# State space branch of a hybrid trunk: y and z with features on partitions instead of tokens

## The chip, the cores and the metric

The kernel runs on one core of one Trainium2 chip. The metric is the device time of one execution in microseconds (us). Three runs of the kernel before the change gave 2074.76, 2075.20 and 2075.37 us, a median of 2075.2.

## The reference

Two layers, each a mixer and a gated feed-forward, over 512 tokens of width 1024 in float32. The mixer has three branches (differential attention, latent attention and a state space branch), which read one normalised input `h`. The change touches the state space branch alone:

```python
xbc = silu(causal_dwconv(xbc, ssm_conv_w, ssm_conv_b))        # xs 1024, bm 4*128, cm 4*128
dt  = softplus(dt_raw + dt_bias);  a = -exp(a_log)            # 16 heads of 64, 4 groups of 4 heads
# per chunk of 128 tokens, cs = cumsum(dt * a) in the chunk
y_diag = ((cm @ bm.T) * exp(cs_l - cs_s) for s <= l) @ (xs * dt)
prev   = state left by the chunks before, decayed
y_off  = (cm @ prev) * exp(cs_l)
ys = y_diag + y_off + ssm_d * xs
ys = rmsnorm_per_group(ys * silu(z)) * ssm_norm               # over the 256 features of a group
# later: merged += sigmoid(gate_c) * (ys @ w_branch_c)
```

## The kernel before, in words

Activations that feed products lie with features on partitions (`hh`, `hl`: 8 tiles of 128 features x 512 tokens). Every float32 product is three products of a high and a low part (`mm3`, L145 to L147). Weights come in blocks of 1024 columns by one load on SP's queue (`wr`), ACT writes the high part (`wh`, L140) and DVE the low part (`wl`, L141); three of each are in turn. `lin_feat` gives a result with features on partitions: 48 wide products of 512 columns for 256 features. `lin_tok` gives it with tokens on partitions: 96 products of 256 columns (L224 to L226).

The branch loops over the 4 groups of heads (`for g in range(SSM_G)`). A group computes, in the order of the text: the x product and its convolution (L877 to L884, three DVE products for a tile, result `cv[0]`, `cv[1]`), the tail of the group before, the product for bm and cm with the same convolution (`cv[2]`, `cv[3]`), the z product, and then:

- `xdt`: x turned to tokens on partitions (L914) times dt; `y` starts as x times ssm_d (L920); bm turned (L926), `cb` = bm times cm (L931, L933), `xte` (L938) and the running states `prev` (L944 to L951)
- for each of 4 heads: the row of cs spread over partitions (L957), `dec` = min, exp (four ACT instructions) and times `cb`, then four y products (L965), one for each chunk of 128 tokens: stationary `dec` of 128 columns, moving `xdt` of 64
- the y products are added to `y`, three off products (L971, 256 columns) are scaled by exp(cs) and added, and `y` is multiplied by the gate of z (L977)
- the squares of `y` are summed along the free axis on ACT (L981), and `rstd_of` (L108 on DVE, L110 a power on POOL) gives one factor per token, that is per partition

The tail (`def tail`) scales `y` by that factor (L986, four instructions), turns `y` with eight transposes on PE (L990) and writes the parts `yh`, `yl` (L993, L994) from PSUM. The tail of group g is called between the x product and the bm and cm product of group g+1, the last one behind the first gate product of the merge.

In this branch a scheduler orders the instructions of each engine by costs of its own. Each engine then takes its queue strictly in that order. Wide products of the next group are put on PE between the small products of this one. Four PSUM banks serve the wide products and four the small ones (`mbank`, `abank`). Behind the branch follows the second attention, whose order on PE is written by hand: query and key products (L1082, L1104), wide products of the merge, and the transposes of queries and keys (L1123), which need DVE's and POOL's normalisation first.

Of the kernel before, what the change touches and what calls it, by code (L numbers as in the profile page):

```python
# [9 lines left out]
F32 = mybir.dt.float32  # L10
# [3 lines left out]
ALU = mybir.AluOpType  # L14
# [51 lines left out]
def trunk_kernel(ctx: ExitStack, tc: tile.TileContext, a: dict, out: bass.AP):  # L66
# [679 lines left out]
    def mix(l, x, hh, hl, ckr, cq, latp, scope):  # L746
# [51 lines left out]
        lss = small([P, T, 2], "lss", 1)  # L798
# [27 lines left out]
        scratch = ssd.tile([P, 256], F32, name="yo", bufs=2).rearrange("p (i t h) -> p i t h", i=4, t=T)  # L826
# [15 lines left out]
        nc.vector.tensor_tensor(out=da, in0=dt, in1=rv["a"].unsqueeze(1).broadcast_to([P, T, SSM_H]), op=ALU.mult)  # L842
        zeros = ssd.tile([P, S], F32, name="cb")
# [3 lines left out]
        cs, ncs, tot, ecs, te = (ssd.tile([P, T, SSM_H], F32, name=nm) for nm in ("cs", "ncs", "tot", "ecs", "te"))  # L847

        def decays():
# [13 lines left out]
            nc.scalar.activation(ecs.rearrange(flat), cp[:, 0:n16], AF.Exp)  # L863
# [6 lines left out]
        with ssd_scope:  # L870
            tails = []
            for g in range(SSM_G):
# [80 lines left out]
                yps = [abank().rearrange("p (c d) -> p c d", c=2) for _ in range(2)]  # L953
                for r in range(4):
                    h = 4 * g + r
                    lp_ = abank()
                    nc.tensor.matmul(lp_, sel[:, h:h + 1].broadcast_to([P, P]), cs_r, start=True, stop=True)  # L957
                    dec = sp.tile([P, T, P], F32, name="dec", bufs=3)
                    nc.vector.tensor_tensor(out=dec, in0=lp_.rearrange("p (c l) -> p c l", c=T),
                                            in1=cs[:, :, h:h + 1].broadcast_to([P, T, P]), op=ALU.min)  # L960
                    for c in range(T):
                        nc.scalar.activation(dec[:, c], dec[:, c], AF.Exp, bias=ncs[:, c, h:h + 1])
                    nc.vector.tensor_tensor(out=dec, in0=dec, in1=cb.rearrange("p (c d) -> p c d", c=T), op=ALU.mult)
                    for c in range(T):
# [623 lines left out]
```

## Time and profile before

| | us |
|---|---|
| median of three runs | 2075.2 |
| the profiled execution | 2072.72 |
| its span | 2071.0 |
| PE busy | 2043.1 |
| DVE busy | 1418.6 |
| ACT busy | 913.8 |
| POOL busy | 137.1 |

A busy PE is not a PE at its peak: its instructions overlap, so that what one costs is read from the distance of starts. The granted clock of TensorE over the span was 0.996. The branch takes two stretches of the span, about 84 to 290 us and about 1100 to 1290 us.

### The profile page before, as it was taken

The numbers are of one execution on the slowest core, as the hardware profiler recorded it, in microseconds if no ns is written. First come the engines' busy times: TensorE is split into PE (matmuls) and PEld (weight loads), VectorE is DVE, ScalarE is ACT, GpSimd is POOL, SyncE is SP. The second block draws the span as 40 slices with busy tenths as digits, with TensorE's granted clock in tenths as the row PEclk, the third lists the DMA queues.
The fourth block names the chain that finished last, engine by engine and source line by source line (L and its number), as shares of the span: only waits on it lengthen the run. The fifth ranks groups of instructions, "written<-read, shape, count | busy, mean of one in ns | idle before, by whom it ended". The sixth has DMA issues, their size and how long they took to land.

```text
span 2071.0 us, 30143 instructions
## 1 busy us (share of the span) xinstructions
PE 2043.1 (99%) x11469; PEld 1769.7 (85%) x11469; DVE 1418.6 (68%) x2742; ACT 913.8 (44%) x1683; POOL 137.1 (7%) x162
## 2 busy tenths in 40 slices
PE   8999999999999999999999999999999999999999
PEld 7888987789888988888898888888998898888888
DVE  7788887756876678658757888775566566553553
ACT  6744445535533454224434544454444335432441
POOL 4200011002100000000000000110020000000000
PEclk8999999999999999999999999999999999999999
DMA  8523232233445255655443223212333243323222
GB/s 268 150 69 85 78 116 90 87 108 113 152 153 169 94 187 165 196 179 166 153 141 85 79 62 89 64 48 79 93 93 93 92 133 92 102 92 102 92 92 82
DMA packets 224542, 237.20 MB, mean 115 GB/s; under 512 B 16126, under 2 KB 195742, under 8 KB 224142
## 3 DMA queue, kind: packets, MB, share of 16 engines
q1 hardware_dynamic: 221646, 232.63, 36.3%
q0 software_dynamic: 2752, 2.65, 0.5%
q8 instruction: 90, 1.47, 0.3%
q14 instruction: 54, 0.44, 0.1%
HBM read 226.30 MB, written 8.91 MB: 114 GB/s over the span
## 4 chain that ended last, share of the span: by engine, by line
PE 87%; DVE 7%; DMA 2%; POOL 2%; issue 2%; ACT 1%; SPq 0%; POOLq 0%; DVEq 0%; ACTq 0%
PE mb L145 22%; PE mb L147 21%; PE mb L146 21%; PE mb L224 3%; PE mb L226 3%; PE mb L225 3%; PE ab L965 1%; DVE wl L141 1%; PE mb L666 1%; PE ab L1140 1%; PE ab L1177 1%; DVE macc L522 1%; PE ab L1326 1%; PE ab L1082 1%; POOL r_r L110 1%
## 5 line engine op out<-in xcount | busy, mean ns | idle before, releaser
L145 PE MATMUL mb<-hh,wh 128*128 128x512 f32 (+1 forms) x1376 | 538.2, 392 | 1.8 <-DVE g L778 0.9
L147 PE MATMUL mb<-hh,wl 128*128 128x512 f32 (+1 forms) x1376 | 532.4, 387 | 0.0
L146 PE MATMUL mb<-hl,wh 128*128 128x512 f32 (+1 forms) x1376 | 531.3, 386 | 0.0
L141 DVE TENSOR_TENSOR wl<-wr,wh 128x1024 fp32r<-128x1024 f32 (+2 forms) x312 | 374.9, 1203 | 193.8 <-ACT wh L140 192.5
L140 ACT ACTIVATE wh<-wr 128x1024 fp32r<-128x1024 f32 (+2 forms) x312 | 324.7, 1042 | 338.4 <-PE mb L146 260.5
L147 PEld LDWEIGHTS mb<-hh,wl 128*128 128x128 f32 x1376 | 258.4, 188 | 51.7
L145 PEld LDWEIGHTS mb<-hh,wh 128*128 128x128 f32 x1376 | 258.3, 188 | 51.8 <-DVE g L778 1.8
L146 PEld LDWEIGHTS mb<-hl,wh 128*128 128x128 f32 x1376 | 258.8, 188 | 49.1 <-DVE hl L702 1.2
L1423 DVE SCALAR_TENSOR_TENSOR fu<-mb,vec,fu 128x510 f32<-128x510 f32 (+1 forms) x176 | 129.8, 745 | 90.5 <-ACT fu L1421 88.9
L224 PE MATMUL mb<-wh,hh 128*128 128x256 f32 x640 | 180.1, 281 | 0.0
L226 PE MATMUL mb<-wh,hl 128*128 128x256 f32 x640 | 178.6, 279 | 0.0
L225 PE MATMUL mb<-wl,hh 128*128 128x256 f32 x640 | 178.5, 279 | 0.0
L145 PE MATMUL mb<-gh,wh 128*128 128x512 f32 (+1 forms) x432 | 151.2, 350 | 0.0
L147 PE MATMUL mb<-gh,wl 128*128 128x512 f32 (+1 forms) x432 | 150.6, 349 | 0.0
L146 PE MATMUL mb<-gl,wh 128*128 128x512 f32 (+1 forms) x432 | 150.5, 348 | 0.0
L1421 ACT ACTIVATE fu<-mb,vec 128x512 f32<-128x512 f32 x88 | 67.9, 774 | 149.7 <-PE mb L147 149.7
L224 PEld LDWEIGHTS mb<-wh,hh 128*128 128x128 f32 x640 | 120.0, 188 | 1.2 <-ACT wh L140 0.4
L225 PEld LDWEIGHTS mb<-wl,hh 128*128 128x128 f32 x640 | 120.1, 188 | 0.4
L226 PEld LDWEIGHTS mb<-wh,hl 128*128 128x128 f32 x640 | 120.2, 188 | 0.0
L522 DVE SCALAR_TENSOR_TENSOR macc<-wg,c_act,macc 128x512 f32<-128x512 f32 x140 | 104.6, 747 | 20.0 <-DMA wg<-in_ada_w_dram 19.2
L145 PE MATMUL mb<-yh,wh 128*128 128x512 f32 x256 | 104.5, 408 | 0.9 <-ACT g L769 0.9
L147 PE MATMUL mb<-yh,wl 128*128 128x512 f32 x256 | 100.3, 392 | 0.0
(333 smaller groups left out, 3373.9 us busy)
## 6 DMA issues: line engine op xcount, KB each, us to landing
wr<-in_w_in_dram SPq DMA_DIRECT2D x88, 512.0 KB
wr<-in_ffn_w_up_dram SPq DMA_DIRECT2D x88, 512.0 KB
wg<-in_ada_w_dram SPq DMA_DIRECT2D x160, 256.0 KB
wr<-in_ffn_w_down_dram SPq DMA_DIRECT2D x40, 512.0 KB
wr<-in_w_in_dram SPq DMA_DIRECT2D x64, 256.0 KB
wm<-in_ada_w_dram SPq DMA_DIRECT2D x16, 512.0 KB
wr<-in_w_branch_c_dram SPq DMA_DIRECT2D x16, 512.0 KB
wr<-in_w_out_dram SPq DMA_DIRECT2D x16, 512.0 KB
```

Source lines behind the costliest of these rows:

```text
L110: nc.gpsimd.tensor_tensor(out=r, in0=ms, in1=nhalf[:, 0:1].broadcast_to([P, n]), op=ALU.pow)
L140: nc.scalar.activation(hi, raw[:, 0:n], AF.Copy)
L141: nc.vector.tensor_tensor(out=lo, in0=raw[:, 0:n], in1=hi, op=ALU.subtract)
L145: nc.tensor.matmul(o, lh, rh, start=first, stop=False)
L146: nc.tensor.matmul(o, lh, rl, start=False, stop=False)
L147: nc.tensor.matmul(o, ll, rh, start=False, stop=last)
L224: nc.tensor.matmul(o, hh[:, kk, ts_], wh[:, sl], start=first and k == 0, stop=False)
L225: nc.tensor.matmul(o, hh[:, kk, ts_], wl[:, sl], start=False, stop=False)
L226: nc.tensor.matmul(o, hl[:, kk, ts_], wh[:, sl], start=False, stop=last and k == 3)
L522: ins = nc.vector.scalar_tensor_tensor(out=acc[0], in0=rk, scalar=c_act[:, kk:kk + 1], in1=acc[0], op0=ALU.mult, op1=ALU.add)
L1421: nc.scalar.activation(u, bank, AF.Identity, bias=v[:, V_FCB + ti:V_FCB + ti + 1], scale=tap(2))
L1423: nc.vector.scalar_tensor_tensor(out=u[:, s_:], in0=bank[:, 0:S - s_], scalar=tap(2 - s_), in1=u[:, s_:], op0=ALU.mult, op1=ALU.add)
```

## The change

- The z product goes through `lin_feat`; `sz` has features on partitions, in one buffer instead of two.
- `y` has features on partitions. It no longer starts from the turned x; ssm_d comes in as a scalar per partition (`dcol`).
- Heads are taken in pairs. Of a y product the stationary side is now `xdt` (64 columns), the moving side `dec` (128 columns); the two heads of a pair write partitions 0 to 63 and 64 to 127 of one bank. The off product has `prev` as its stationary side, six products of 128 columns for three of 256. exp(cs) is taken from the spread row (`grow`).
- The factor of the norm is per token, which is now the free axis. The squares are summed over partitions by four products with a column of ones; the factor, again one per token with tokens on partitions, is written to DRAM (`r_d`, 512 numbers of 4 bytes) and read back spread over all partitions (`rows_`, 256 KB), both by POOL's queue. The second load waits for the first.
- The tail multiplies `y` by `rows_` and the norm's weight and splits it. It has no transposes.
- A few small tiles are made larger, so that tiles behind them keep their places.

```diff
@@ -840,11 +840,16 @@
+        dcol = ssd.tile([P, 64], F32, name="dcol")[:, 0:SSM_H // 2]
+        for r in range(2):
+            own = slice(r * SSM_HD, (r + 1) * SSM_HD)
+            nc.vector.tensor_copy(out=dcol[own], in_=rv["dvec"][own].rearrange("p (j r) -> p j r", r=2)[:, :, r])
...
@@ -898,28 +902,24 @@
-                sz = sp.tile([P, T, 256], F32, name="sz", bufs=2)
-
-                def ev_z(tt, bank):
-                    o = sz[:, 2 * tt:2 * tt + 2]
+                sz = sp.tile([P, 2, S], F32, name="sz")
+
+                def ev_z(i, bank):
+                    o = sz[:, i]
                     nc.scalar.activation(o, bank, AF.Tanh, scale=0.5)
                     nc.vector.scalar_tensor_tensor(out=o, in0=o, scalar=1.0, in1=bank, op0=ALU.add, op1=ALU.mult)
-                lin_tok(w_in, [(C_Z + 256 * g, 256)], hh, hl, ev_z)
+                lin_feat(w_in, (C_Z + 256 * g, C_Z + 256 * g + P), KT, h_rhs, ev_z)
...
-                    nc.vector.tensor_tensor(out=y[:, :, sl].rearrange("p c (r d) -> p c r d", r=2), in0=tv,
-                                            in1=rv["dvec"][:, hs].unsqueeze(1).unsqueeze(3).broadcast_to([P, T, 2, SSM_HD]),
-                                            op=ALU.mult)
...
@@ -950,48 +950,58 @@
-                for r in range(4):
...
-                    for c in range(T):
-                        nc.tensor.matmul(yps[c // 2][:, c % 2, r * SSM_HD:(r + 1) * SSM_HD], dec[:, c],
-                                         xdt[:, c, r * SSM_HD:(r + 1) * SSM_HD], start=True, stop=True)
+                for i in range(2):
+
+                    dec = sp.tile([P, 2, S], F32, name="dec", bufs=2)
+                    grow = sp.tile([P, S], F32, name="yo", bufs=2)
+                    for r in range(2):
...
+                        nc.tensor.matmul(lp_, sel[:, h:h + 1].broadcast_to([P, P]), cs_r, start=True, stop=True)
...
+                        nc.scalar.activation(grow[own, P:S], lp_[own, P:S], AF.Exp)
...
+                    nc.vector.tensor_tensor(out=dec, in0=dec, in1=cb.unsqueeze(1).broadcast_to([P, 2, S]), op=ALU.mult)
+                    yp = abank()
                     for c in range(T):
...
+                        for r in range(2):
+                            own = slice(r * SSM_HD, (r + 1) * SSM_HD)
+                            nc.tensor.matmul(yp[own, cs_], xdt[:, c, i * P + r * SSM_HD:i * P + (r + 1) * SSM_HD], dec[:, r, cs_],
+                                             start=True, stop=True)
+                    op_ = abank()
+                    for c in range(1, T):
+                        cs_ = slice(c * P, (c + 1) * P)
+                        nc.tensor.matmul(op_[:, cs_], prev[:, c - 1, i * P:(i + 1) * P], cmT[:, cs_], start=True, stop=True)
+                    nc.vector.tensor_tensor(out=grow[:, P:S], in0=grow[:, P:S], in1=op_[:, P:S], op=ALU.mult)
+                    j = 2 * g + i
+                    nc.vector.scalar_tensor_tensor(out=y[:, i], in0=cv[i], scalar=dcol[:, j:j + 1], in1=yp, op0=ALU.mult, op1=ALU.add)
+                    nc.vector.tensor_tensor(out=y[:, i, P:S], in0=y[:, i, P:S], in1=grow[:, P:S], op=ALU.add)
+                nc.vector.scalar_tensor_tensor(out=y, in0=y, scalar=0.5, in1=sz, op0=ALU.mult, op1=ALU.mult)
+                sq = [sp.tile([P, S], F32, name="yo", bufs=2) for _ in range(2)]
                 for i in range(2):
...
+                    nc.scalar.activation(sq[i], y[:, i], AF.Square)
+                nc.vector.tensor_tensor(out=sq[0], in0=sq[0], in1=sq[1], op=ALU.add)
+                ssp = abank()
                 for c in range(T):
-                    jk = sp.tile([P, 256], F32, name="yo", bufs=2)
-                    nc.scalar.activation(jk, y[:, c], AF.Square, accum_out=ss[:, c:c + 1])
-                r_ = rstd_of(ss, T, 256.0, "yn")
+                    nc.tensor.matmul(ssp[:, c:c + 1], sq[0][:, c * P:(c + 1) * P], ones[:, 0:1], start=True, stop=True)
+                r_ = rstd_of(ssp[:, 0:T], T, 256.0, "yn")
+
+                r_d = dram.tile([1, S], F32, name=f"r_d{l}{g}")
+                nc.gpsimd.dma_start(out=r_d.rearrange("o (c p) -> p (o c)", p=P), in_=r_)
+                rows_ = sp.tile([P, S], F32, name="u", bufs=3)
+                nc.gpsimd.dma_start(out=rows_, in_=r_d.broadcast_to([P, S]))
+
+                def tail(g=g, y=y, rows_=rows_):
                     for i in range(2):
-                        tp = abank()
-                        for c in range(T):
-                            nc.tensor.transpose(out=tp[:, c * P:(c + 1) * P], in_=y[:, c, i * P:(i + 1) * P], identity=ident)
+                        cw = col(V_SN + 2 * g + i)
+                        nc.vector.scalar_tensor_tensor(out=y[:, i], in0=y[:, i], scalar=cw, in1=rows_, op0=ALU.mult, op1=ALU.mult)
                         yh, yl = y_tiles()
...
+                        nc.scalar.activation(yh, y[:, i], AF.Copy)
+                        nc.vector.tensor_tensor(out=yl, in0=y[:, i], in1=yh, op=ALU.subtract)
                         ys.append((yh, yl))
```

How the instructions stand, at three places. DVE, first layer, from the gating of `y` of the first group to its tail (`u`, `cv`: convolution of the next group; `yn_ms`: input of the power on POOL; `yl`: low part of the result). Before:

```order
L977 SCALAR_TENSOR_TENSOR y<-y,sz 128x1024 [waits DVE_49]
L879 SCALAR_TENSOR_TENSOR u<-mb,vec_89,u 128x511 [waits Activation_49] x2
L879 SCALAR_TENSOR_TENSOR u<-mb,vec_89,u 128x510 [waits DVE_49]
L108 TENSOR_SCALAR yn_ms<-yss 128x4 [waits Activation_49]
L879 SCALAR_TENSOR_TENSOR u<-mb,vec_89,u 128x510 [waits DVE_49]
L879 SCALAR_TENSOR_TENSOR u<-mb,vec_89,u 128x509 [waits DVE_49] x2
L986 TENSOR_SCALAR y<-y,yn_r 128x256 [waits Pool_49]
L884 SCALAR_TENSOR_TENSOR cv<-cv,u 128x512 [waits Activation_49]
L986 TENSOR_SCALAR y<-y,yn_r 128x256 x3
L884 SCALAR_TENSOR_TENSOR cv<-cv,u 128x512 [waits Activation_49]
L141 TENSOR_TENSOR wl<-wr,wh 128x1024 [waits DMAHW3_49,PE_49]
L994 SCALAR_TENSOR_TENSOR yl<-ab,vec_89,yh 128x512 [waits Activation_49] x2
```

And now, where L1001 is the product of the tail (its `u` is the buffer of `rows_`) and DMASW the queue of POOL's loads:

```order
L983 SCALAR_TENSOR_TENSOR y<-y,sz 128x1024 [waits DVE_49]
L987 TENSOR_TENSOR yo<-yo 128x512 [waits Activation_49]
L108 TENSOR_SCALAR yn_ms<-ab 128x4 [waits PE_49]
L141 TENSOR_TENSOR wl<-wr,wh 128x1024 [waits DMAHW5_49,Activation_49]
L883 SCALAR_TENSOR_TENSOR u<-mb,vec_89,u 128x511 [waits Activation_49] x2
L883 SCALAR_TENSOR_TENSOR u<-mb,vec_89,u 128x510 [waits DVE_49] x2
L883 SCALAR_TENSOR_TENSOR u<-mb,vec_89,u 128x509 [waits DVE_49] x2
L1001 SCALAR_TENSOR_TENSOR y<-y,vec_89,u 128x512 [waits DMASW1_49]
L888 SCALAR_TENSOR_TENSOR cv<-cv,u 128x512 [waits Activation_49] x2
L1004 TENSOR_TENSOR yl<-y,yh 128x512 [waits Activation_49]
L1001 SCALAR_TENSOR_TENSOR y<-y,vec_89,u 128x512
```

Six convolution products and one `wl` stand between the norm's input L108 and the first instruction that waits for the load; the convolutions' second halves and the parts `yl` stand behind it.

POOL's queue in the first layer, before:

```order
L110 TENSOR_TENSOR lat_r<-lat_ms,nhalf 128x8 [waits DVE_49]
L110 TENSOR_TENSOR yn_r<-yn_ms,nhalf 128x4 [waits DVE_49] x3
L110 TENSOR_TENSOR yn_r<-yn_ms,nhalf 128x4 [waits DVE_49,Pool_49]
L1134 AFFINE_SELECT cmask<-sb 128x512 [waits DMAHW1_49,DMAHW2_49,DVE_49,PE_49]
L110 TENSOR_TENSOR r_r<-r_ms,nhalf 128x4 [waits DVE_49] x3
```

Now:

```order
L110 TENSOR_TENSOR lat_r<-lat_ms,nhalf 128x8 [waits DVE_49]
L110 TENSOR_TENSOR yn_r<-yn_ms,nhalf 128x4 [waits DVE_49]
L994 DMA r_d_1698<-yn_r 128x4x1 [waits DMASW0_49,Pool_49]
L996 DMA u<-r_d_1698 128x512 [waits DMASW1_49,DMAHW6_49,DMASW0_49,Activation_49]
L110 TENSOR_TENSOR yn_r<-yn_ms,nhalf 128x4 [waits DVE_49]
```

Behind each power stand the write to DRAM and the load from it, and the load waits for the write.

DVE behind the last group of the first layer, where the second attention begins (`Cq`: a table of the rotation). Before:

```order
L108 TENSOR_SCALAR yn_ms<-yss 128x4 [waits Activation_49]
L986 TENSOR_SCALAR y<-y,yn_r 128x256 [waits Pool_49]
L986 TENSOR_SCALAR y<-y,yn_r 128x256 x3
L141 TENSOR_TENSOR wl<-wr,wh 128x1024 [waits DMAHW3_49,PE_49,Activation_49]
L994 SCALAR_TENSOR_TENSOR yl<-ab,vec_89,yh 128x512 [waits Activation_49] x2
L1043 TENSOR_TENSOR Cq<-cos,w32q 128x4x16
```

Now:

```order
L108 TENSOR_SCALAR yn_ms<-ab 128x4 [waits PE_49,Pool_49]
L522 SCALAR_TENSOR_TENSOR macc<-wg,c_act,macc 128x512 [waits DMAHW7_49,DVE_49]
L141 TENSOR_TENSOR wl<-wr,wh 128x1024 [waits DMAHW4_49,PE_49,Activation_49]
L522 SCALAR_TENSOR_TENSOR macc<-wg,c_act,macc 128x512 [waits DMAHW1_49,DVE_49]
L522 SCALAR_TENSOR_TENSOR macc<-wg,c_act,macc 128x512 [waits DMAHW2_49,DVE_49]
L1001 SCALAR_TENSOR_TENSOR y<-y,vec_89,u 128x512 [waits DMASW7_49]
L1001 SCALAR_TENSOR_TENSOR y<-y,vec_89,u 128x512
L1004 TENSOR_TENSOR yl<-y,yh 128x512 [waits Activation_49] x2
L1053 TENSOR_TENSOR Cq<-cos,w32q 128x4x16
```

The wait for POOL alone has become a wait for POOL's load, and the attention's work on DVE stands behind it.

## Rows read from the trace of the kernel before

**Rows 1.** The page, busy time of each engine, its share, instructions.

```profile
PE 2043.1 (99%) x11469; PEld 1769.7 (85%) x11469; DVE 1418.6 (68%) x2742; ACT 913.8 (44%) x1683; POOL 137.1 (7%) x162
```

**Rows 2.** Windows, one group: us, busy (instructions) of each engine, PEclk, DMA share, GB/s.

```profile
170.78:214.12 43.34, 43.34 (x269) 38.81 (x268) 36.63 (x60) 21.02 (x44) 1.38 (x1) 1.00 0.27 74
```

**Rows 3.** The chain in order of time (start us, us, what), first layer.

```profile
126.14 0.87 PE ab L914 x8
170.78 0.87 PE ab L914 x8
175.85 1.29 PE ab L944 x6
214.12 0.87 PE ab L914 x8
```

**Rows 4.** Timeline of PE (start us, us, line, out<-in, shapes), the same group.

```profile
180.42 1.00 PE L965 MATMUL ab<-xdt,dec 128*128 128x64 f32 x8
189.42 0.39 PE L145 MATMUL mb<-hh,wh 128*128 128x512 f32 x1
...
198.53 0.39 PE L146 MATMUL mb<-hl,wh 128*128 128x512 f32 x1
202.65 0.28 PE L224 MATMUL mb<-wh,hh 128*128 128x256 f32 x1
208.30 0.28 PE L224 MATMUL mb<-wh,hh 128*128 128x256 f32 x1
```

**Rows 5.** Timeline of PE, products on column halves in the second attention.

```profile
344.79 1.09 PE L1177 MATMUL ab<-pT,vv 128*64 128x128 f32 x16
345.81 1.13 PE L1104 MATMUL ab<-wm,lat 128*128 128x256 f32 x4
```

**Rows 6.** Timeline of PE, sums over partitions by products with ones.

```profile
696.20 0.28 PE L147 MATMUL mb<-mh,wl 128*128 128x256 f32 x1
696.68 0.36 PE L145 MATMUL mb<-mh,wh 128*128 128x256 f32 x1
```

**Rows 7.** Timeline of DVE in the same group.

```profile
175.85 1.22 DVE L141 TENSOR_TENSOR wl<-wr,wh 128x1024 fp32r<-128x1024 f32 x1
188.89 1.29 DVE L968 TENSOR_TENSOR y<-y,ab 128x512 f32<-128x512 f32 x2 [1.88 <-PE ab L965]
196.37 0.16 DVE L108 TENSOR_SCALAR yn_ms<-yss 128x4 f32<-128x4 f32 x1
198.03 0.35 DVE L986 TENSOR_SCALAR y<-y,yn_r 128x256 f32<-128x256 f32 x1 [0.24 <-POOL yn_r L110]
205.05 2.71 DVE L879 SCALAR_TENSOR_TENSOR u<-mb,vec,u 128x510 f32<-128x510 f32 x4
210.74 0.69 DVE L884 SCALAR_TENSOR_TENSOR cv<-cv,u 128x512 f32<-128x512 f32 x1
```

**Rows 8.** The instructions of two tiles: bias_d, then c.

```profile
L670 POOL DMA_DIRECT2D bias_d<-ob x16: 691/735/938, 18.6 to 71.5; - x16
DMA to landing us min/median/max: 4.2/5.8/14.7
...
L474 SPq DMA_DIRECT2D c<-in_c_dram x1: 406/406/406, 0.8 to 0.8; - x1
L476 PEld LDWEIGHTS ab<-ident,c x1: 178/178/178, 2.4 to 2.4; 8*128 8x128 f32 x1
```

**Rows 9.** Timeline of PE, then DVE, behind the last group, first layer.

```profile
275.79 0.48 PE L147 MATMUL mb<-hh,wl 128*128 128x512 f32 x1
303.18 0.42 PE L1123 MATMUL ab<-ident,kn 128*96 128x128 f32 x2 [0.63 <-DVE kn L1116]
...
287.69 0.21 DVE L1043 TENSOR_TENSOR Cq<-cos,w32q 128x64 f32<-128x64 f32 x1
289.93 1.75 DVE L522 SCALAR_TENSOR_TENSOR macc<-wg,c_act,macc 128x512 f32<-128x512 f32 x2
```

**Rows 10.** Windows, a stretch ahead of the branch.

```profile
40.00:48.00 8.00, 5.58 (x26) 4.82 (x25) 7.93 (x22) 6.01 (x15) 4.57 (x5) 0.80 0.66 180
```

More of the change, by code (lines that the diff above doesn't have):

```diff
@@ L795, in mix @@
         sp = ssd = ssd_scope.enter_context(tc.tile_pool(name=f"ssd{l}", bufs=1, reuse_waits="tile"))
-        lss = small([P, T, 2], "lss", 1)
+        lss = small([P, 8 * T], "lss", 1)[:, 0:2 * T].rearrange("p (t k) -> p t k", k=2)
         krss = small([P, T], "krss", 2)
@@ L825, in mix @@
         dt = ssd.tile([P, T, SSM_H], F32, name="dt")
-        scratch = ssd.tile([P, 256], F32, name="yo", bufs=2).rearrange("p (i t h) -> p i t h", i=4, t=T)
+        scratch = ssd.tile([P, S], F32, name="yo", bufs=2)[:, 0:256].rearrange("p (i t h) -> p i t h", i=4, t=T)
         e, z2, poly = scratch[:, 0], scratch[:, 1], scratch[:, 2]
@@ L846, in mix @@
         nc.vector.tensor_copy(out=cs_r, in_=zeros)
-        cs, ncs, tot, ecs, te = (ssd.tile([P, T, SSM_H], F32, name=nm) for nm in ("cs", "ncs", "tot", "ecs", "te"))
+        cs, ncs, tot, te = (ssd.tile([P, T, SSM_H], F32, name=nm) for nm in ("cs", "ncs", "tot", "te"))
         def decays():
@@ L914, in mix @@
                         nc.tensor.transpose(out=tp[:, c * P:(c + 1) * P], in_=cv[i][:, c * P:(c + 1) * P], identity=ident)
-                    tv = tp.rearrange("p (c r d) -> p c r d", c=T, r=2)
                     hs = slice(4 * g + 2 * i, 4 * g + 2 * i + 2)
-                    sl = slice(i * P, (i + 1) * P)
-                    nc.vector.tensor_tensor(out=xdt[:, :, sl].rearrange("p c (r d) -> p c r d", r=2), in0=tv,
+                    nc.vector.tensor_tensor(out=xdt[:, :, i * P:(i + 1) * P].rearrange("p c (r d) -> p c r d", r=2),
+                                            in0=tp.rearrange("p (c r d) -> p c r d", c=T, r=2),
                                             in1=dt[:, :, hs].unsqueeze(3).broadcast_to([P, T, 2, SSM_HD]), op=ALU.mult)
-                    nc.vector.tensor_tensor(out=y[:, :, sl].rearrange("p c (r d) -> p c r d", r=2), in0=tv,
-                                            in1=rv["dvec"][:, hs].unsqueeze(1).unsqueeze(3).broadcast_to([P, T, 2, SSM_HD]),
-                                            op=ALU.mult)
                 bmt = sp.tile([P, T - 1, P], F32, name="bmt")
@@ L967, in mix @@
-                for i in range(2):
-                    nc.vector.tensor_tensor(out=y[:, 2 * i:2 * i + 2], in0=y[:, 2 * i:2 * i + 2], in1=yps[i], op=ALU.add)
-                for c in range(1, T):
-                    op_ = abank()
-                    nc.tensor.matmul(op_[:, 0:256], cmT[:, c * P:(c + 1) * P], prev[:, c - 1], start=True, stop=True)
-                    yo = sp.tile([P, 256], F32, name="yo", bufs=2)
-                    nc.vector.tensor_tensor(out=yo.rearrange("p (r d) -> p r d", r=4),
-                                            in0=op_[:, 0:256].rearrange("p (r d) -> p r d", r=4),
-                                            in1=ecs[:, c, hd].unsqueeze(2).broadcast_to([P, 4, SSM_HD]), op=ALU.mult)
-                    nc.vector.tensor_tensor(out=y[:, c], in0=y[:, c], in1=yo, op=ALU.add)
```

28 lines of the change are left out of this document (9 added, 19 removed).

## The prediction

> **What bounds the kernel now.** I began with the busy times of the engines: the reader is to see that PE is busy 99% of the span and no other engine more than 68% [rows 1]. Then I cut out one group of heads of the first layer. In its 43.34 us PE is busy for 43.34, DVE for 36.63, ACT for 21.02 and POOL for 1.38, at a granted clock of 1.00 [rows 2]. The chain of waits confirms it: from one turn of x (L914) to the next, the chain consists of PE alone, and the distance is 44.64 us to the second group and 43.34 to the third [rows 3]. So each microsecond less on PE is a microsecond of time, as long as nothing else becomes late, and DVE, which works 85% of the group, is the first that could.
>
> **What the change saves on PE**, per group, in steps.
> - The turns of y: eight transposes. Eight of the same shape (L914) take 0.87 [rows 3]. Saved: 0.87.
> - The z product: 96 products of 256 columns become 48 of 512. Of the former, 48 lie between 202.65 and 208.30, 0.1177 each, so 11.30 in all. Of the latter, 40 lie between 189.42 and 198.53, 0.228 each, so 10.93 [rows 4]. Saved: 0.37.
> - The block of y products runs from 180.42 to 189.42 [rows 4] and holds 15 wide products and three spread rows of cs, which are as wide: 18 x 0.228 = 4.10. The remaining 4.90 are y and off products. In their place come two sets of eight products on the two column halves. The second attention has eight of this kind: 344.79 to 345.81, that is 1.02 [rows 5], so 2.04. Six off products of 128 columns stand for three of 256: I take the six of L944, 1.29 [rows 3]. With 0.4 for changes of form between them that is 3.73. Saved: 1.17.
> - The sums of squares: four products with ones. In the normalisation of the feed-forward such sums stand between products 0.48 apart (696.20 to 696.68) that take 0.12 without them, so 0.36 [rows 6]. I count it twice, for the return to wide products. Added: 0.72.
>
> That is 1.7 less for a group, about 41.65 instead of 43.34. With eight groups it would be −13.5, if nothing waited. DVE loses its two products with ssm_d and some small pieces (about 1.4 of 36.6 per group), and ACT gains about 0.8 by the exps of the spread row; it has half of the group free [rows 2], which hides that.
>
> **What the change adds: a way through DRAM.** Before, the factor is ready for its user on DVE 1.66 after the norm's input (L108 at 196.37, L986 at 198.03 [rows 7]). Now, behind the same power on POOL, come a write to DRAM, a load that waits until it has landed, and then L1001 on DVE. On DVE's queue L1001 stands ahead of the second halves of the convolutions of the next group's bm and cm, of both parts of y, of the z gate, of xdt and of xte. PE needs bm's convolution for L926 and xte for L944. So if the load comes late, DVE stands, and after it PE.
>
> How late is late? Let D be the two landings together, from the write's issue to the load's arrival, and let time zero be the end of the last y product.
> - Off products (0.64), twenty wide products (4.55) and a hop of 0.1 bring PE to the sums at 5.3. They end at 6.1, L108 starts at 6.25, the power is done at 7.9, and the rows are there at 7.9 + D.
> - DVE's six convolution products and a low part of weights behind L108 take 6 x 0.67 + 1.15 (four of L879 in 2.71, a last one being 0.7; wl 1.22 with its overlap [rows 7]), so DVE reaches L1001 at 11.4. It waits from D = 3.5 on.
> - From L1001 to the end of xte stand 13 products of 512 columns at 0.60 (two in 1.29, one alone 0.69 [rows 7]), six of the convolution, 4.0, one low part, 1.15, and three pieces of xte, 1.05 (a piece of 256 columns takes 0.35 [rows 7]): 14.0. So xte is ready at 21.9 + D, with a hop 22.0 + D.
> - Then PE has, up to the next time zero: L944 1.29, two spread rows and hop 0.55, 24 wide 5.47, the first y products 1.02, off products 0.64, spread rows 0.55, 24 wide 5.47, hop 0.1, y products 1.02: 16.1.
>
> The period is the longer of 41.65 and 38.1 + D. It costs nothing up to D = 3.5, and is worse than 43.34 from D = 5.2 on.
>
> **How large is D?** No transfer of before goes to DRAM and straight back. The nearest row is POOL's other write of small blocks, bias_d: sixteen of them land 4.2 us after issue at the least, 5.8 in the middle, 14.7 at most [rows 8], at the start of the kernel, where the DMA engines are 0.66 busy (180 GB/s [rows 10]). In a group they are 0.27 busy (74 GB/s [rows 2]). So I take the least twice: D = 8.4. From below, the nearest row is the first transfer of SP: c, issued at 0.8 and used at 2.4 [rows 8], at most 1.6, on idle engines, for a few rows; twice that is 3.2. From above, the median of bias_d twice is 11.6. Less than nothing it can't be, since the load waits for the write.
>
> The Trainium skill (DMA: Bandwidth & Descriptors, section "Anatomy of one DMA — SWDGE (gpsimd) path") gives a transfer issued by POOL a fixed part of about 2.0 us and the bytes at 436 GB/s on top; for 2 KB and 256 KB that is an estimate of 2.0 + 2.6 = 4.6, and the period would be 42.7, shorter than before, the time 2069. The landings of bias_d in this trace are at least twice its fixed part, so I hold to them; the other case is the first rival.
>
> **The sum.** With D = 8.4 the period is 46.5: +1.9 at the first boundary (44.64) and +3.2 at each of the other two, +8.3 for a layer. The first group gains its share before time zero, −1.6. Behind the last group it is the attention that waits: PE's L1123 needs the keys, and the whole chain on DVE that makes them, from the rotation's tables at 287.69 to 303.18 [rows 9], now stands behind L1001. Before, L1123 came 27.4 after the last y product (275.79). Now 29 wide products stand ahead of the sums, so L108 is at 8.3, the power at 9.95, the rows at 9.95 + D, the tail takes 2.7, and the chain 12.0 (15.5 less two `macc`, 1.75, and two low parts, 1.7, which have moved ahead or aside): 24.65 + D, +5.7 at D = 8.4. PE would reach L1123 at about 22 and wait some 11. Together +12.4 a layer, 4D − 21.3 in general, and even at D = 5.3. Two layers: +24.8.
>
> The profiled execution took 2072.72 (span 2071.0), 2.5 below the median of the three runs. 2072.72 + 24.8 = 2097.5, on the median 2100.
>
> Costed at nothing: POOL's queue stands while it waits between its two transfers, but POOL has 1.38 us of work in a group, the power itself; only the norms of the attention's queries and keys stand behind it, and these wait for DVE anyway. The issue on POOL (0.7 a transfer [rows 8]) lies inside the landing times. SP loads the same bytes of z's weights in the same number of loads.
>
> **Rivals.**
> - Quick landing, D under 4.8. For it: the loads in the group have nearly idle DMA engines. Against it: bias_d. At D = 3.2 the layer gives −1.66 for three periods, −1.6 for the first group and about +0.5 for the attention's chain: −6.1, in all −12, 2063. It decides below D = 5.3.
> - Even, D from 4.8 to 5.8: the gain on PE and the new wait cancel, within 4 us, 2075.
> - The clock falls in the new gaps. With D = 8.4 PE stands for some 3 us ahead of L926 and 1 ahead of L944 in each group. In an early stretch PE is busy 5.58 of 8 us and the granted clock is 0.80 [rows 10], 1.6 us lost. For it: gaps of about the size. Against: two gaps in 46 us are less than there. One such loss for each of the eight waits, 13 us more: 2113.
> - The column halves don't run beside each other here. Two sets of eight cost 1.02 more each, 16 us in all: 2116. The attention's eight [rows 5] speak against it.
>
> **How the numbers follow.** Forecast 0.45, quick landing 0.23, even 0.10, the clock 0.18, the halves 0.04. Within 0.2% (4 us, about what a measurement of this kernel can tell from no change) is the even case, 0.10; faster is the first rival, 0.23; the rest is slower, 0.67. The range goes from the low bound of D to the high one: 4 x 11.6 − 21.3 = +25.1 a layer, +50, 2125, a little more for the clock: 2064 to 2128. With the forecast alone (D from 6.5 to 11) it is 2085 to 2121.
>
> **What would show it.** The wait of DVE at L1001 for the load, D − 3.5 = 4.9 us in each of six groups, longer in the last ones; waits of PE at L926 for `cv` and at L944 for `xte`, together about 4.8; one of some 11 at L1123 for `kn` in each layer; the period of L914 at 46.5. On the side of the gain: eight y products in 1.02, wide z products 0.228 apart, the sums in 0.72. I am wrong if the write and the load land within 5 us together, or if L1001 waits and PE does not, because the scheduler's order gives it enough to do.

## The result and the profile after

| | us | ratio to before | 95% interval |
|---|---|---|---|
| before | 2074.98 | | |
| after | 2170.05 (2168.49 to 2171.58, four runs) | 1.0459 | 1.0441 to 1.0477 |

The change makes the kernel 95 us slower; 25 were forecast, and the range ended at 2128. The profiled execution took 2169.62, 96.9 more than that of before. The page of after begins with PE, as in [rows 1]:

```profile
PE 2056.7 (95%) x11133; PEld 1751.9 (81%) x11133; DVE 1412.1 (65%) x2690; ACT 922.1 (43%) x1665; POOL 150.8 (7%) x178
```

PE is busy 13.6 us longer than before and stands 83 us more: the loss is waiting. Where it waits is read by stretches of the first layer, from the end of the last y product of one group to that of the next, and from the last one to the first turn of the queries (window, length, busy time of PE, PEld, DVE, ACT, POOL, granted clock, DMA share, GB/s):

```profile
146.41:199.37 52.96, 45.76 (x240) 37.58 (x238) 35.90 (x53) 23.92 (x45) 3.35 (x3) 0.94 0.25 65
199.37:253.02 53.65, 44.83 (x226) 36.36 (x224) 35.73 (x53) 22.07 (x42) 2.40 (x3) 0.90 0.23 64
253.02:307.91 54.89, 45.73 (x228) 36.61 (x226) 35.18 (x53) 23.15 (x44) 3.35 (x3) 0.91 0.22 63
307.91:350.93 43.02, 24.89 (x111) 20.88 (x110) 20.90 (x54) 8.75 (x15) 7.48 (x8) 0.76 0.40 96
```

Three periods of 52.96, 53.65 and 54.89 stand where one took 43.34 (44.64 the first) [rows 2, 3], and the end takes 43.02 where it was 25.9 (275.8 to 301.7). PE is idle for 7 to 9 us of each period and for 18 of the end, and the granted clock is below 1.00 in every one.

At the boundaries between groups the mechanism is the one forecast. Timeline of DVE at the first boundary (start us, duration us, what; in brackets the idle time before and who ended it):

```profile
168.47 0.75 DVE L1001 SCALAR_TENSOR_TENSOR y<-y,vec,u 128x512 f32<-128x512 f32 x1 [8.20 <-DMA u<-r_d]
181.48 1.08 DVE L938 TENSOR_TENSOR xte<-xdt,te 128x256 f32<-128x256 f32 x3
```

L1001 waits 8.20 us for the load, and from its start to the end of `xte` (182.5) go 14.1 us; 14.0 were forecast from [rows 7]. PE behind it, at the turn of bm and at the running states:

```profile
178.12 0.88 PE L926 MATMUL ab<-ident,cv 128*128 128x128 f32 x3 [6.34 <-DVE cv L888]
182.96 1.46 PE L944 MATMUL ab<-xte,bmt 128*128 128x256 f32 x6
```

PE waits at L926 for the convolution, as foreseen, and not at L944: DVE's last piece of `xte` ends just ahead of it. The steps of the boundary are those forecast; what differs is D, the time from the write's issue to the rows' arrival. The new way on POOL:

```profile
155.43 0.83 POOL L994 DMA_DIRECT2D r_d<-yn_r  x1 [0.29 <-POOL yn_r L110]
164.19 0.59 POOL L996 DMA_DIRECT2D u<-r_d  x1 [7.92 <-DMA r_d<-yn_r]
```

The write is issued at 155.43, the load, when the write has landed, at 164.19, and L1001 starts at 168.47: D is 13.0. Over all eight groups, instructions and landing times of the write (L994) and the load (L996):

```profile
L994 POOL DMA_DIRECT2D r_d<-yn_r x8: 801/806/833, 155.4 to 1372.7; - x8
DMA to landing us min/median/max: 8.2/9.0/10.6
...
L996 POOL DMA_DIRECT2D u<-r_d x8: 556/558/586, 164.2 to 1383.8; - x8
DMA to landing us min/median/max: 3.9/4.3/7.3
```

The load lands in 4.3, near the 4.2 that I took from bias_d [rows 8]. The write, of 2 KB, needs 9.0. In the six boundaries D is 13.0 to 14.0 (8.4 forecast, 11.6 the upper bound). For most of the write's time the trace records no packet, of it or of anything else: the last one ends at 157.63, and the write lands at 163.6. The packets from 157.7 to 164:

```profile
DMA packets 0, 0.00 MB, mean 0 GB/s; under 512 B 0, under 2 KB 0, under 8 KB 0
```

What passes in those 6 us no run shows. The trace may not record every piece on POOL's way, since e2_16byte, with a quarter of the pieces, has as many packets; e3_sp, on SP's, shows the pieces themselves.

The end of the branch, first layer. POOL's timeline:

```profile
318.62 0.81 POOL L994 DMA_DIRECT2D r_d<-yn_r  x1 [0.29 <-POOL yn_r L110]
329.71 0.56 POOL L996 DMA_DIRECT2D u<-r_d  x1 [10.28 <-issue]
```

SP's queue, from a pair of loads `wg` to the first of `wm`:

```profile
321.94 4.76 SPq L512 DMA_DIRECT2D wg<-in_ada_w_dram  x2
326.75 3.42 SPq L1078 DMA_DIRECT2D wm<-in_mla_w_uq_dram  x1
```

DVE, at the tail of the last group:

```profile
337.04 1.41 DVE L1001 SCALAR_TENSOR_TENSOR y<-y,vec,u 128x512 f32<-128x512 f32 x2 [14.34 <-DMA u<-r_d]
```

PE, from the last y products to the turn of the queries (the last line is the first product of the attention in the second layer):

```profile
306.89 1.09 PE L973 MATMUL ab<-dec,xdt 128*64 128x128 f32 x16
307.92 0.94 PE L978 MATMUL ab<-cv,prev 128*128 128x128 f32 x6
308.61 0.48 PE L147 MATMUL mb<-hh,wl 128*128 128x512 f32 x1
315.44 1.02 PE L990 MATMUL ab<-ones,yo 128*128 128x1 f32 x8
316.32 0.47 PE L146 MATMUL mb<-hl,wh 128*128 128x512 f32 x1
337.24 2.93 PE L1092 MATMUL ab<-wm,lat 128*128 128x192 f32 x8 [18.13 <-DMA wm<-in_mla_w_uq_dram]
350.93 0.60 PE L1133 MATMUL ab<-ident,qn 128*96 128x128 f32 x4
1387.76 2.93 PE L1092 MATMUL ab<-wm,lat 128*128 128x192 f32 x8 [13.77 <-DMA wm<-in_mla_w_uq_dram]
```

Here D is 18.4, the write 11.1 us to the load's issue and the load 7.3. The rotation's tables, DVE's first work for the attention, stand at 339.76, behind it. PE, too, waits, already at its first product of the attention, for `wm`. In the first layer the loads of `wm` stand on SP behind a pair of `wg`, issued over 4.76 us. That is not all of it: in the second layer no `wg` stands there, `wm` is issued at 1376.60, and PE can start 11.2 us later. The write was then on its way (issued at 1372.66, landed at 1383.2). In e2_16byte, told below, the load at this place serves PE 5.0 us after its issue (1332.39 to 1337.43). Windows behind the two issues, after first:

```profile
1378.00:1384.00 6.00, 0.00 (x0) 0.00 (x0) 0.00 (x0) 0.00 (x0) 0.21 (x1) 0.50 0.38 31
1333.00:1337.00 4.00, 0.00 (x0) 0.00 (x0) 0.01 (x1) 0.00 (x0) 0.00 (x0) 0.50 0.93 270
```

While the write of 4-byte pieces was pending, all transfers together moved 31 GB/s (11 in the first layer, 324 to 330), and 204 once it had landed. So the slow write seems to delay PE here in a second way, which the prediction did not have. This is inferred from the times; how a pending write would hold the loads back is not shown.

Behind each gap the clock is low. Windows at the second boundary:

```profile
226.00:230.00 4.00, 0.00 (x0) 0.00 (x0) 4.00 (x7) 1.60 (x3) 0.00 (x0) 0.52 0.00 0
230.00:234.00 4.00, 2.69 (x12) 2.62 (x13) 4.00 (x6) 2.55 (x5) 0.00 (x0) 0.50 0.50 132
```

In the first of them PE does nothing; when it starts again (231.31) it runs at 1.2 GHz, which the clock column gives as 0.50.

### The profile page after: what moved, and what is told of

The parts are those of the page before. It is cut to its first block, busy times and chain, and to the rows that moved or that the text cites. A ratio compares the mean times of both kernels' runs of the same rounds, so it can differ in the third digit from the quotient of the medians.

```text
span 2167.6 us, 29483 instructions
## 1 busy us (share of the span) xinstructions
PE 2056.7 (95%) x11133; PEld 1751.9 (81%) x11133; DVE 1412.1 (65%) x2690; ACT 922.1 (43%) x1665; POOL 150.8 (7%) x178
## 3 DMA queue, kind: packets, MB, share of 16 engines
q0 software_dynamic: 3648, 4.76, 1.0%
## 4 chain that ended last, share of the span: by engine, by line
PE 67%; DVE 9%; DMA 4%; issue 2%; POOL 2%; ACT 1%; POOLq 0%; DVEq 0%; ACTq 0%; SPq 0%
PE mb L145 18%; PE mb L147 18%; PE mb L146 18%; DMA r_d<-yn_r 2%; PE mb L224 1%; PE mb L226 1%; PE mb L225 1%; DVE wl L141 1%; DMA wg<-in_ada_w_dram 1%; DMA u<-r_d 1%; PE ab L1150 1%; PE ab L1187 1%; POOL r_r L110 1%; PE ab L1336 1%; DVE macc L522 1%
## 5 line engine op out<-in xcount | busy, mean ns | idle before, releaser
L145 PE MATMUL mb<-hh,wh 128*128 128x512 f32 (+1 forms) x1504 | 588.8, 392 | 3.7 <-DVE u L883 1.3
L146 PE MATMUL mb<-hl,wh 128*128 128x512 f32 (+1 forms) x1504 | 582.6, 387 | 0.0
L147 PE MATMUL mb<-hh,wl 128*128 128x512 f32 (+1 forms) x1504 | 581.9, 387 | 0.0
L145 PEld LDWEIGHTS mb<-hh,wh 128*128 128x128 f32 x1504 | 284.4, 189 | 62.7 <-issue 2.9
L224 PE MATMUL mb<-wh,hh 128*128 128x256 f32 x384 | 108.3, 282 | 0.0
L225 PE MATMUL mb<-wl,hh 128*128 128x256 f32 x384 | 107.1, 279 | 0.0
L226 PE MATMUL mb<-wh,hl 128*128 128x256 f32 x384 | 107.0, 279 | 0.0
L146 PE MATMUL mb<-yl,wh 128*128 128x512 f32 x256 | 100.0, 390 | 0.0
L146 PEld LDWEIGHTS mb<-gl,wh 128*128 128x128 f32 x432 | 81.5, 189 | 10.6
L147 PEld LDWEIGHTS mb<-gh,wl 128*128 128x128 f32 x432 | 81.1, 188 | 10.7
```

The costliest lines, as they stand in the source:

```text
L145: nc.tensor.matmul(o, lh, rh, start=first, stop=False)
L146: nc.tensor.matmul(o, lh, rl, start=False, stop=False)
L147: nc.tensor.matmul(o, ll, rh, start=False, stop=last)
L224: nc.tensor.matmul(o, hh[:, kk, ts_], wh[:, sl], start=first and k == 0, stop=False)
L225: nc.tensor.matmul(o, hh[:, kk, ts_], wl[:, sl], start=False, stop=False)
L226: nc.tensor.matmul(o, hl[:, kk, ts_], wh[:, sl], start=False, stop=last and k == 3)
```

## The experiments

All were run beside the kernel before; the last column is the ratio to it.

| run | edit to after | us | ratio (95%) |
|---|---|---|---|
| e1_pe_spread | spread by PE, no DRAM | 2105.1 | 1.0146 (1.0131 to 1.0162) |
| e2_16byte | 128 pieces of 16 bytes | 2118.4 | 1.0210 (1.0193 to 1.0227) |
| e4_late | tails later | 2143.4 | 1.0326 (1.0311 to 1.0342) |
| e6_fill | 26 idle products, 48 rows | 2193.5 | 1.0571 (1.0555 to 1.0587) |
| e7_own | own buffer for the rows | 2162.1 | 1.0423 (1.0402 to 1.0444) |
| e8_own_late | e7 and e4 | 2120.8 | 1.0228 (1.0206 to 1.0250) |
| e11_own_spread | e7 and e1 | 2092.2 | 1.0094 (1.0075 to 1.0113) |
| e12_fill_full | 26 idle products, 128 rows | 2185.3 | 1.0534 (1.0517 to 1.0551) |
| e13_hybrid | e2, e7, e4; last group e1 | 2089.2 | 1.0060 (1.0048 to 1.0073) |
| e14_hybrid_early | e13 without e4 | 2109.0 | 1.0158 (1.0144 to 1.0172) |
| e10_own_late_spread | e11 and e4 | 2103.3 | 1.0129 (1.0116 to 1.0143) |
| e3_sp | both transfers on SP | 2179.3 | 1.0499 (1.0483 to 1.0516) |

**The way through DRAM: e2_16byte, e3_sp, e1_pe_spread.**

```diff
-nc.gpsimd.dma_start(out=r_d.rearrange("o (c p) -> p (o c)", p=P), in_=r_)
+nc.gpsimd.dma_start(out=r_d.rearrange("o (p c) -> p (o c)", c=T), in_=r_)      # e2: and the tail reads rows_ with stride T
```

> The changed kernel, but the write to DRAM puts the four factors of a partition side by side (128 pieces of 16 bytes instead of 512 of 4), and the tail reads the row with a stride of four. Theory C (the write takes 8.5 us because of its 512 pieces): it lands in 4 to 5 us like the load, D falls from 13 to about 9, and with 4D a layer the time falls by 30, to 2130 to 2145. Rival D (the landing is a fixed price of a write by this queue): it stays at 8 to 9 us and the time at 2165 to 2172.

52 us less. Write and load as above:

```profile
L994 POOL DMA_DIRECT2D r_d<-yn_r x8: 606/606/638, 157.2 to 1328.4; - x8
DMA to landing us min/median/max: 1.9/2.7/3.3
...
L996 POOL DMA_DIRECT2D u<-r_d x8: 538/548/569, 160.3 to 1332.1; - x8
DMA to landing us min/median/max: 3.4/3.6/5.6
```

And PE's waits (us in total, times, longest), which were 31.9 and 40.8 in after:

```profile
PE ab L1092 <- DMA wm<-in_mla_w_uq_dram: 18.9, 2, 11.2
PE ab L926 <- DVE cv L888: 13.3, 6, 3.2
```

The write fell from 9.0 to 2.7 with a quarter of the pieces and the same bytes: theory C holds. The edit makes the pieces fewer and larger at once, so which of the two counts is not separated; spread over the pieces saved, the fall is (9.0 - 2.7) / 384 = 16 ns each, an estimate. The time fell by more than theory C's 30, since D fell from 13.5 to 6.9 in the boundaries and by 10.3 and 7.5 at the two ends: 6 x 6.6 + 17.8 = 57 by the prediction's sum.

```diff
-nc.gpsimd.dma_start(out=r_d...      -nc.gpsimd.dma_start(out=rows_...
+nc.sync.dma_start(out=r_d...        +nc.sync.dma_start(out=rows_...       # e3
```

> The changed kernel with both transfers issued by SP instead of POOL, still 512 pieces of 4 bytes. Theory M (the pieces cost in the DMA engines, whoever issues): the write lands in 8 to 9 us as before, SP's loads of weights stand behind the waits, and the time is 2165 to 2200. Rival N (the price is that of POOL's queue, which makes a descriptor for each piece): the write lands in 2 to 4 us and the time falls to 2110 to 2140.

2179, the time of theory M. SP's queue at the first boundary, and the packets of all queues from 155.5 to 156:

```profile
154.67 0.37 SPq L994 DMA_DIRECT2D r_d<-yn_r  x1
164.50 0.34 SPq L996 DMA_DIRECT2D u<-r_d  x1
```

```profile
DMA packets 528, 0.00 MB, mean 4 GB/s; under 512 B 528, under 2 KB 528, under 8 KB 528
```

The load can go only when the write has landed, 9.8 us after its issue here and 8.2 to 11.1 in the eight groups: with 4-byte pieces SP's queue is no quicker than POOL's, and rival N is out. But theory M's reason, a cost of the pieces in the DMA engines, is not what this trace shows: the 528 small packets, the 512 pieces among them, pass the engines within half a microsecond, and the load goes 8.6 us after that. What the write waits for then is open.

```diff
-r_d = ...; nc.gpsimd.dma_start(...); rows_ = ...; nc.gpsimd.dma_start(...)
+rb = abank()
+for c in range(T):
+    nc.tensor.matmul(rb[:, c * P:(c + 1) * P], r_[:, c:c + 1].broadcast_to([P, P]), ident, start=True, stop=True)
+rows_ = sp.tile([P, S], F32, name="u", bufs=3)
+nc.scalar.activation(rows_, rb, AF.Copy)                                     # e1
```

> The changed kernel, but the factor of the norm reaches all partitions by four products on PE (factor spread as the stationary side, identity moving) and one copy by ACT; no write to DRAM and no load. Theory A (the way through DRAM is the whole loss): DVE no longer waits for a load, PE no longer stands at L926, the granted clock of the branch is back at 1.00, the period of a group is 41.7 plus 0.5 for the spread, and the time is 2075 - 13.5 + 4 = 2066, 2056 to 2078. Rival B (part of the loss is the new order itself: the loads of the attention's first weights wm stand on SP's queue behind four loads wg): PE still waits at the attention's first product for wm, some 10 to 18 us in each layer, and the time is 2085 to 2105.

2105: neither. 65 of the 95 us were the way through DRAM, but without it the kernel is still 30 slower than before, and not for B's reason (PE waits 1.5 us in all for `wm`; with the way gone SP's order was another). DVE at the second boundary:

```profile
202.00 1.41 DVE L1002 SCALAR_TENSOR_TENSOR y<-y,vec,u 128x512 f32<-128x512 f32 x2 [2.97 <-ACT u L997]
203.33 4.02 DVE L883 SCALAR_TENSOR_TENSOR u<-mb,vec,u 128x511 f32<-128x511 f32 x6
```

PE at the same place, from the spread (L995) to its next wide product:

```profile
200.21 1.12 PE L995 MATMUL ab<-ident,yn_r 128*128 128x128 f32 x8
206.84 0.47 PE L145 MATMUL mb<-hh,wh 128*128 128x512 f32 x1 [2.52 <-DVE u L883]
```

DVE still stands 2.97 us at the tail (L1002), now for POOL, PE and ACT. Only then come all six convolution products of the next group, and PE waits for them. Over the whole run PE also waits 9.0 us, in six places, for POOL's power at the spread.

**The buffer: e7_own, e4_late, e8_own_late, e11_own_spread.** In after the load's target is one of the three `u` of the convolutions. The products of bm and cm need that buffer, so the order puts them behind the tail; in before, some of x's convolution, too, stood ahead of the norm's input, and now all of it stands behind.

```diff
-rows_ = sp.tile([P, S], F32, name="u", bufs=3)
+rows_ = sp.tile([P, 2, S], F32, name="dec", bufs=2)[:, 0]                    # e7, e8, e11
```

> The changed kernel with one edit: the spread factors lie in a buffer of dec instead of one of the three buffers u of the convolutions. Theory I (in the changed kernel the load takes a buffer that the next group's bm and cm convolutions need, so that all of them stand behind the tail on DVE): with three buffers free, more of the convolution runs ahead of the tail, DVE has about 11 us of work behind it instead of 14, and the time falls by 3 to 4 in each of six boundaries: 2145 to 2155. Rival J (the ring of u is no cause; the landing alone sets the period): 2165 to 2172.

2162, 8 us less, between the two. The second and third period fell to 50.6 and 50.5, the first did not.

```diff
-if tails: tails.pop()()                       # behind the x product
+if tails: tails.pop()(prev[:, T - 2, 0:1])    # behind the running states; the column of weights is made from it: prev * 0 + cw   # e4, e8
```

> The changed kernel with the same two transfers, but in groups 2 to 4 the tail of the group before is bound to the end of the running states (its column of weights is made from the last of prev), so that its first instruction stands on DVE some 13 us later; the tail of the last group is as before. Theory E (what costs is DVE standing at the tail with the next group's work behind it): no wait in the six boundaries, period about 41.7, saved 3 x 11 to 13 in each layer, the ends unchanged: 2095 to 2110. Rival F (the transfers themselves disturb the weights' loads or POOL): the time stays above 2140.

> The same with the tail in groups 2 to 4 bound to the end of the running states, as in e4_late. Theory I: e4_late kept a wait because the load held a buffer u until the late tail; without that the six boundaries wait for nothing, the period is PE's own work, 42.5 to 43.5, and the ends are as in the changed kernel: 2170 - 2 x 32 = 2106, 2100 to 2116. Rival K (e4_late lost its time by the order of ACT and DVE that comes with a late tail): 2135 to 2146 again.

e4_late missed theory E by 33 us. PE's waits in it:

```profile
PE mb L145 <- DVE u L883: 23.6, 6, 5.6
```

No wait at L926 is left, but the load now holds its `u` until the late tail, and PE waits 23.6 us for the convolutions (L883). The time alone is rival F's, above 2140; e8_own_late, with the same transfers, answers it. With the buffer free these waits are gone and 20 to 23 us with them (by the ratios and by the times). It stayed 5 above I's range: in its profile, of an execution of 2129, PE still waits 7.9 us in four places for `xte` and, as in after, 32.2 for `wm`.

> e1_pe_spread with the factors in a buffer of dec. Theory I: e1_pe_spread lost its 30 us because its convolutions too stood behind the tail (PE waited 2.5 us for them, and the clock fell behind that); with the buffers free the period is PE's work, 43.4 with the spread, plus up to 1.8 where PE waits for POOL's power: 2076 to 2090. Rival L (the spread's own place in PE's queue costs it): 2100 to 2106 as in e1_pe_spread.

2092, just above I's range: the buffer was worth 11 to 13 us here. Of the 18 that are left, PE's own wait for POOL's power at the spread is about half, 9.4 in the profile, which is of an execution of 2101:

```profile
PE ab L995 <- POOL yn_r L110: 9.4, 8, 1.8
```

**The clock: e6_fill, e12_fill_full.** Both add products that nobody reads.

```diff
 lin_feat(w_in, (C_Z + 256 * g, C_Z + 256 * g + P), KT, h_rhs, ev_z)
+if g > 0:
+    fb = abank()
+    for q in range(26):
+        nc.tensor.matmul(fb, sel[0:48, 0:1].broadcast_to([48, P]), cs_r[0:48], start=True, stop=True)    # e6
+        nc.tensor.matmul(fb, hh[:, 0, 0:P], hh[:, 0], start=True, stop=True)                             # e12
```

> The changed kernel with more work: in groups 2 to 4 of each layer 26 products of 512 columns that nobody reads (0.227 each, 5.9 us) stand behind the z product, mostly just where PE waits for the convolutions. Theory G (behind each gap of 7 us PE runs at half clock for 2.5 to 5 us, which costs some 2 us a gap beside the gap itself): the gap shrinks to about 2 us, the granted clock there stays near 1.00, and the kernel is faster with more work, by 6 to 12 us: 2158 to 2164. Rival H (the clock in the rows costs nothing there, since something else sets the pace behind the gap): the time stays at 2170 or rises.

23 us slower than after. PE's timeline at the first boundary, the fillers:

```profile
170.25 6.37 PE L915 MATMUL ab<-cs_r,sel 48*128 48x512 f32 x21
```

The window of their second half:

```profile
174.00:178.00 4.00, 4.00 (x14) 2.96 (x13) 4.00 (x7) 3.18 (x5) 0.00 (x0) 0.50 0.18 43
```

PE is busy without a pause, and the clock, 0.97 from 170 to 174, is 0.50 here. The time is as rival H has it, not as theory G; but since the fillers themselves brought the low clock, the run decides between neither.

> e6_fill with other fillers: 26 products of 512 columns that nobody reads, now with all 128 rows (a part of h as the stationary side, h moving) instead of 48. In e6_fill the granted clock fell to 0.50 while the 48-row products ran without a pause. Theory G2: with 128 rows it stays at 1.00, and PE leaves the stretch at full speed; how much time that gives back depends on who ends last there: if PE, 1 to 2 us a boundary, 2158 to 2165; if DVE's chain from the tail to xte, nothing, 2167 to 2173. Rival H2 (rows make no difference): clock 0.50 in the fill again and 2185 to 2196 as in e6_fill.

15 us slower than after. PE's timeline at the same place, the fillers and the next states:

```profile
169.95 4.93 PE L915 MATMUL ab<-hh 128*128 128x512 f32 x21
182.74 0.67 PE L948 MATMUL ab<-xte,bmt 128*128 128x256 f32 x2 [3.76 <-DVE xte L942]
```

Two windows, in the fill and behind the wait:

```profile
172.00:176.00 4.00, 3.75 (x21) 2.99 (x19) 4.00 (x6) 1.61 (x4) 0.00 (x0) 1.00 0.00 0
184.00:188.00 4.00, 4.00 (x13) 3.18 (x12) 2.29 (x6) 0.45 (x2) 0.00 (x0) 0.66 0.12 43
```

With these fillers the clock stayed at 1.00 in the fill, as G2 says. But the time is H2's (2185 to 2196), without H2's sign: PE then waited 3.76 us at L948 for `xte`, and the clock fell there (0.66). In this order DVE, busy without a pause from 167.4 to 184, has three low parts of weights ahead of `xte` where after has one, and `xte` ends 16.5 us behind the tail's start instead of 14.1. So e12 compares another order of DVE as well. What the clock itself costs in after was not settled by these two.

**Together: e13_hybrid, e14_hybrid_early, e10_own_late_spread.**

> All that the runs so far point to, together: groups 1 to 3 write 16-byte pieces and read them back into a buffer of dec, their tails bound to the end of the running states; group 4, behind which nothing can hide the way, spreads its factor by PE. Theory I with C: no boundary waits, the period is PE's work, 42.7 to 43.0, and the end is as before plus 1: 2075 - 3 + 2 = 2074, 2068 to 2084. Rival (PE's saving was as large as forecast, 1.7 a group): 2060 to 2067. Rival (a late load of the weights, as e8_own_late had once, stays): 2085 to 2095.

> The same without binding the tails: they stand on DVE where the scheduler puts them. With the write at 2.7 and the load at 3.6 us the way takes 7, and the buffers of the convolutions are free. Theory I: DVE waits 1 to 3 us at the tail but has less behind it, PE waits 0 to 2 a boundary: 2074 to 2090. Rival (the early tail alone costs as much as in e2_16byte, whose end cost some 7 a layer): 2095 to 2105.

> e11_own_spread with the tails bound to the end of the running states. Theory: DVE's wait for the spread in e11_own_spread goes, PE's wait of 1.4 us for POOL's power at the spread stays, eight times, and PE's work is 43.4: 2080 to 2090. Rival (no gain over e11_own_spread): 2090 to 2096.

e13_hybrid is the best, 2089.2, still 13 us above before: the rival with the late load, not theory I. Windows of its second and third period:

```profile
193.79:235.93 42.14, 41.98 (x227) 34.64 (x225) 36.41 (x56) 22.14 (x42) 3.08 (x3) 1.00 0.31 82
235.93:278.25 42.32, 41.89 (x226) 34.17 (x224) 35.72 (x55) 21.76 (x42) 3.09 (x3) 1.00 0.29 82
```

PE at its end:

```profile
298.42 2.93 PE L1105 MATMUL ab<-wm,lat 128*128 128x192 f32 x8 [8.12 <-DMA wm<-in_mla_w_uq_dram]
311.40 0.60 PE L1146 MATMUL ab<-ident,qn 128*96 128x128 f32 x4
```

The periods are 42.14 and 42.32 with PE idle for 0.2 to 0.4 us: here at last one sees what the change saves, 1.0 to 1.2 us of 43.34 (PE is busy 1.4 less). The first period, 44.75, saves nothing on its 44.64. The first layer's end costs 33.2 from 278.25 where it was 25.9, and 8.12 of it is the wait for `wm`, the late load, which stands at the end and not in a period; the second layer's end, 25.2, loses nothing. Between the two profiles (16.5 us apart) the first branch with its end loses 6.4 and the second 1.0; about 9 lie outside both, some 3 of them ahead of the first branch, in stages that the change does not touch. Their cause is open. The tails must be late: without that (e14, above both of its ranges) PE waits 16.5 us at L931 for the convolutions. e10, which should have gained on e11, lost 7 to 11 (by the ratios and by the times); its profile shows PE's wait for POOL unchanged (8.7 in all) and 8.0 for `wm`, and I did not take it further. No version beats the kernel before.

## Why the prediction was wrong

The side was right, the size not: +25 forecast, +95 measured. The step that failed is D, the landing of the write and the load.

- **The landing of the write was mis-sized.** "The nearest row is POOL's other write of small blocks": I took its time and called it small, without asking in how many pieces r_d goes. D = 8.4 was 13.0 to 14.0 in the boundaries (13.5 in the mean) and 18.4 and 16.1 at the two ends. Put into the prediction's own sum, the first layer's periods become 38.1 + 13.0 = 51.1 and 52.1 twice, and the end 24.65 + 18.4 = 43.05. Measured are 52.96, 53.65, 54.89 and 43.02. For two layers that is 6 x 5.1 + 10.0 + 7.7 = 48 of the 72 us that were missing; e2_16byte shows it from the other side. Of the rest, 13 lie in periods longer than the sum, about 6 in the first groups, about 3 outside the branches. The upper bound, the median of bias_d twice, bounded nothing, since that row doesn't say in how many pieces its blocks go.
- **The clock, a rival, came beside the forecast, at a price that is not shown.** It falls to 0.50 behind every gap. With the measured D the six periods of both layers are 1.4 to 3.0 above the sum, 13.2 in all, and 1.6 a gap, from [rows 10], looks like it. By legs it is not so simple. From time zero to the write's issue go 8.3 to 9.2 us for the 7.9 forecast, 5.6 more in all, and from L1001 to the end of `xte` 14.1 four times and 15.2 twice, with one more low part of weights on DVE, 2.8 more. Only the last leg, from there to the next time zero, holds the low clock on PE's own path: 16.0 to 18.0 for the 16.2 forecast, 4.8 more. So the clock can be at most about 4.8 of the 13.2.
- **PE's saving was 1.4 a group, not 1.7, and 1.0 to 1.2 of it reached the period** (e13_hybrid). The y products on column halves cost 1.02 to 1.03 a set, as [rows 5] said (306.89 to 307.92). The off products take 0.69 a set of six passes (307.92 to 308.61), 1.38 in all for 1.29. The sums take 0.88 (315.44 to 316.32), not the 0.36 of [rows 6] twice, 0.72. That is 0.25 of the missing 0.3. The first group reached its time zero later, not 1.6 earlier (146.41; 144.44 before). But 163 wide products (512 columns each, halves counted as such) stand ahead of it from 100 us on, where before had 144: the order moved them forward from the end, some 4 us of work at 0.23 each, so the later time hides a gain of about 2.
- **A part of the change was not priced.** The diff shows that the load goes into one of the three `u`, and I didn't follow who else needs them: the buffer costs 8 us beside the slow landing (e7_own), 20 to 23 where the tail is late (e8 to e4) and 11 to 13 without DRAM (e11 to e1).
- **The end** came out right in length, in part by luck. The sum runs to the turn of the keys, and with the measured D it gives 43.05 and 40.75 for the two layers; they took 43.8 and 40.6. But PE stood at L1092 for `wm`, 18.13 us, and not some 11 at L1133 for the keys. From L1092 on, PE has 13.7 us of its own work to the keys, and DVE needs 14.6 from L1001 to the last of them: in the first layer the load of `wm` (337.24) and the rows (337.04) came together, so that the two paths end within 0.2 us of each other, and in the second PE waits 0.76 for the keys. The path through `wm` was not in the prediction. With the way gone (e1) the end takes 25.95, as before: the order of SP's loads moved with it, and no slow write was pending.
- The Trainium skill (DMA: Bandwidth & Descriptors, section "Anatomy of one DMA — SWDGE (gpsimd) path") gave 2.0 us for the write and 2.6 for the load. The write in 128 pieces took 2.7 and the load 3.6 (e2), the write in 512 pieces 9.0: its rule by bytes comes near here for the 128 pieces of 16 bytes and not for the 512 of 4.

## What to carry to other kernels

Before you price a small transfer, ask in how many pieces it goes and how large they are: 2 KB as 512 numbers took three times as long as 2 KB in 128 pieces, and one index written in another order was worth 52 us. Look, too, at what else is loaded while it is pending. When a product moves behind a transfer, follow its target's buffer as well as its queue: what shares the buffer ring waits too. And a saving on the busiest engine is worth nothing until the in-order engine beside it no longer waits for it.

## What was not expected of the hardware

- Writes of 4-byte pieces from 128 partitions to DRAM: 512 of them landed 8.2 to 10.6 us after issue by POOL's queue, and by SP's queue the load that waits for them went 8.2 to 11.1 us after; 128 pieces of 16 bytes landed in 1.9 to 3.3 (POOL's queue). On SP's queue the pieces had passed the DMA engines 8.6 us before that load went (e3_sp, first boundary). At the ends of the branch all transfers together moved 11 to 31 GB/s while such a write was pending and loads of weights were issued, and 204 once it had landed.
- TensorE's clock fell to its lower level while products with 48 rows ran without a pause for 6 us (0.50 in 174 to 178), and stayed at the upper one through as many with 128 rows (1.00 in 172 to 176).
